# Lower parts of the second FFN's down weights: a negated ScalarE copy and an adding DMA in place of a VectorE subtraction

## The chip, the core and the metric

The kernel runs on one core of a Trainium2 chip. The metric is the device time of one execution in microseconds; lower is better. Three runs of the kernel before took 2208.71, 2209.5 and 2211.62 us; the median is 2209.5 us.

## What is computed

One layer of a diffusion backbone over 1024 latent tokens of width 1024, with 256 context tokens beside them: a half-step SwiGLU feed-forward, a parallel mixer (neighbourhood attention and an S5 scan), and a second half-step SwiGLU feed-forward. The last of these is what the change touches:

```
def swiglu(h, w_up, w_down):
    a, g = jnp.split(h @ w_up, 2, axis=-1)
    return (jax.nn.silu(g) * a) @ w_down
...
x = post_norm(x, 0.5 * mod[8] * swiglu(modulate(x, mod[6], mod[7]), ffn2_w_up, ffn2_w_down), ln_g[2], ln_b[2])
```

The hidden width is 2816, that is 22 blocks of 128; `w_down` is 2816 by 1024.

## The kernel before

TensorE multiplies in fp32r, and the kernel keeps float32 accuracy by writing each operand as an upper part (the value rounded to fp32r) and a lower part (what the rounding left). Each product of two such operands is three matmuls: upper by upper, upper by lower, lower by upper.

Weights arrive by DMA in units of 128 by 1024 (512 KB, tile `ws`). SP issues the loads; units rotate through three buffers (`NWS = 3`), and a buffer is loaded again once both of its halves have been split. A half (128 by 512) is an item. `w_split` makes its parts: ScalarE copies it into `wh` as fp32r (line 259), VectorE subtracts `wh` from the source into `wl` (line 261). `wh` and `wl` come from rings of four buffers. `take(n)` hands the next n items to TensorE and calls `w_split` so that `ahead[0]` items (normally four) are split, as far as the ring has room; then `w_next` issues the weight loads that have become possible. All of it is written in program order: every engine works its own list in order, and SP's list holds the loads and the stores of everything.

The down projection of the second feed-forward has 88 items, numbers `DOWN` to `DOWN + 87`, in two parts.

- Its first part works tokens 0 to 511. All eight PSUM banks accumulate (four token blocks by two halves of the columns). Each of the 22 hidden blocks takes two items and is 24 matmuls (lines 1793 to 1795: `h` by `wh`, `h` by `wl`, `l` by `wh`). The last two blocks go together, and four of their items have buffers of their own (`XE`). While it runs, SP also loads the hidden activations of both halves of the tokens (`hid_load`, line 1705), residual rows (line 1756) and rows of the norm (line 471). `take` for a block splits the two items of the block after it, since the ring has only four places.
- Its second part works tokens 512 to 1023 with `token_major`: first one half of the columns, then the other, one item and 12 matmuls a block (lines 397 to 399). During its first blocks VectorE finishes the first part: `updated` (lines 1771, 1772), the statistics (lines 420 to 426), the power on GpSimd (line 427), the norm (lines 436, 1776, 1777), after which SP stores the rows (line 1778). The last eight blocks of the second half of the columns go together (`TAIL = 8`), token block by token block; five of their items have buffers of their own (`XE`, `A`). Each token block is then finished at once and stored (lines 1771 to 1815).

GpSimd does almost nothing: 33 instructions in the whole kernel, in this stage only the powers of line 427. It issues no DMA.

Of the kernel before, what the change touches and what calls it, by code (L numbers as in the profile page):

```python
# [11 lines left out]
F32 = mybir.dt.float32  # L12
F32R = mybir.dt.float32r
I32 = mybir.dt.int32
AF = mybir.ActivationFunctionType
ALU = mybir.AluOpType
# [32 lines left out]
def hybrid_layer(ctx: ExitStack, tc: tile.TileContext, I, out, dbg=None, stop=99):  # L49
# [3 lines left out]
    V, S, G = nc.vector, nc.scalar, nc.gpsimd  # L53
# [12 lines left out]
    def nm(s):  # L66
        cnt[0] += 1
        return f"{s}_{cnt[0]}"
# [72 lines left out]
    units, items, last_use = [], [], {}  # L141
# [60 lines left out]
    DOWN = len(items)  # L202
# [23 lines left out]
    def w_dma(n):  # L226
        while pos[0] < min(n, len(units)):
            assert w_next(0)
# [3 lines left out]
    ready = {}  # L232


    def source(i, need=True):
        if i not in ready and i < len(items):
            u, f = items[i]
            if not need and (u >= pos[0] or i < U_ITEMS or i >= DOWN):
                return
            w_dma(u + 1)  # L240
            ready[i] = f()
        return ready.get(i)

    def w_split(n, must):
        while pos[1] < min(n, len(items)):
            i = pos[1]
            if i not in apart and len(ringed) >= 4:
                assert i >= must, i
                break
            if items[i][0] >= barred[0] and i >= must:  # L250
                break
            src = source(i)
            if i in apart:
                wh, wl = apart.pop(i)
            else:
                ringed.add(i)
                wh = wp.tile([128, 512], F32R, name=nm("wh"), tag="wh", bufs=4)
                wl = wp.tile([128, 512], F32R, name=nm("wl"), tag="wl", bufs=4)
            S.activation(wh, src, AF.Copy)  # L259
            source(i + 1, False)  # L260
            V.tensor_tensor(wl, ready.pop(i), wh.bitcast(F32), op=ALU.subtract)  # L261
            wsp[i] = (wh, wl)
            pos[1] += 1


    def take(n=1):
        i = pos[2]
        pos[2] += n
        for j in list(ringed):
            if j < i:  # L270
                ringed.discard(j)
        w_split(i + max(n, ahead[0]), i + n)
        while w_next(2):
            pass
        return [wsp.pop(j) for j in range(i, i + n)]
# [232 lines left out]
    for k in range(KD):  # L508
        if k + 2 < KD:
            k_load(k + 2)  # L510
        w_dma((2, 3, 4, 4, 4, 4, 5, 6)[k])
        for m in range(2):
            mod_tile(ws1.pop(0), m, k, True, False)
        if k == 0:
            for m in (1, 4, 7):
                V.tensor_scalar(bada[:, m], bada[:, m], 1.0, None, op0=ALU.add)
        V.tensor_tensor(modl[:, 0:2, k], modl[:, 0:2, k], bada[:, 0:2, k], op=ALU.add)
        if rest_of is not None:
            rest_of()
        w_split((0, 2, 4, 6, 8, 8, 8, 8)[k], 0)  # L520
        if k:
            grow(k - 1, (0, 1, 2, 3, 4, 4, 4, 4)[k])
        xt = xs.pop(0)
        S.activation(xt, xt, AF.Identity, scale=modl[:, 1, k:k + 1], bias=modl[:, 0, k:k + 1])
        S.activation(X[0][k], xt, AF.Copy)
        rest_of = lambda k=k, xt=xt: V.tensor_tensor(X[1][k], xt, X[0][k].bitcast(F32), op=ALU.subtract)
    rest_of()
    grow(KD - 1, 4)
    for i in range(8):
        wsp.pop(i)  # L530
    pos[2] = 8
    w_split(12, 0)
    started = ((pb8[0], pb8[1]), (pb8[2], pb8[3]))
    c_row(1)
# [1248 lines left out]
    for f in range(NF - LAST + 1):  # L1783
# [4 lines left out]
        for t in range(4):  # L1788
            for i in range(n):
                h, l = hidden(f + i, t)  # L1790
                for hf in range(2):
                    wh, wl = ws[2 * i + hf]
# [106 lines left out]
```

## Time and profile before

| | us |
|---|---|
| median of three runs | 2209.5 |
| lowest and highest run | 2208.71, 2211.62 |
| profiled execution, its own time | 2211.69 |
| profiled execution, span from the first to the last instruction | 2209.6 |
| TensorE busy in the span | 2154.9 (98%) |
| VectorE busy | 1597.0 (72%) |
| ScalarE busy | 739.1 (33%) |

The profiled execution lasts 2.1 us longer than its span and 2.2 us longer than the median of the runs. A matmul of 512 columns is listed with 0.39 us, but a new one starts every 0.227 us, since they are pipelined; the starts give the pace. The granted TensorE clock is a share of full speed.

### The profile page before, as it was taken

The numbers are of one execution on the slowest core, as the hardware profiler recorded it, in microseconds if no ns is written. First come the engines' busy times: TensorE is split into PE (matmuls) and PEld (weight loads), VectorE is DVE, ScalarE is ACT, GpSimd is POOL, SyncE is SP. The second block draws the span as 40 slices with busy tenths as digits, with TensorE's granted clock in tenths as the row PEclk, the third lists the DMA queues.
The fourth block names the chain that finished last, engine by engine and source line by source line (L and its number), as shares of the span: only waits on it lengthen the run. The fifth ranks groups of instructions, "written<-read, shape, count | busy, mean of one in ns | idle before, by whom it ended". The sixth has DMA issues, their size and how long they took to land. (4 is left out here: it accounts for less than half of the span.)

```text
span 2209.6 us, 32479 instructions
## 1 busy us (share of the span) xinstructions
PE 2154.9 (98%) x12272; PEld 1933.3 (87%) x12272; DVE 1597.0 (72%) x3425; ACT 739.1 (33%) x1547; POOL 22.0 (1%) x33
## 2 busy tenths in 40 slices
PE   6999999999999999999999999999899999999998
PEld 6998899889998999898899899986688888888786
DVE  7888878798887887553777466788877777744845
ACT  4322223423322223324222367634433333332121
POOL 0000000000000000000000000000000000000000
PEclk9999999999999999999999999999999999999999
DMA  9787723436433444433877675244223333279442
GB/s 353 251 291 258 268 67 109 161 100 237 128 124 117 126 135 128 137 125 128 274 252 248 179 175 136 81 168 162 103 108 114 115 114 115 96 266 390 168 150 83
DMA packets 169612, 372.31 MB, mean 169 GB/s; under 512 B 18152, under 2 KB 85736, under 8 KB 166640
## 3 DMA queue, kind: packets, MB, share of 16 engines
q1 hardware_dynamic: 169456, 370.25, 49.6%
q8 instruction: 96, 1.57, 0.3%
q14 instruction: 60, 0.49, 0.1%
HBM read 292.09 MB, written 84.06 MB: 170 GB/s over the span
## 5 line engine op out<-in xcount | busy, mean ns | idle before, releaser
L337 PE MATMUL pb<-X,wh 128*128 128x256 f32 (+2 forms) x1744 | 558.2, 320 | 0.9 <-ACT wh L259 0.9
L339 PE MATMUL pb<-X,wl 128*128 128x256 f32 (+2 forms) x1744 | 555.8, 319 | 0.0
L261 DVE TENSOR_TENSOR wl<-ws,wh 128x512 fp32r<-128x512 f32 x456 | 304.1, 688 | 246.8 <-ACT wh L259 241.3
L259 ACT ACTIVATE wh<-ws 128x512 fp32r<-128x512 f32 x456 | 278.7, 627 | 563.3 <-PE pb L399 288.0
L337 PEld LDWEIGHTS pb<-X,wh 128*128 128x128 f32 x1744 | 330.7, 190 | 9.6 <-ACT wh L259 1.3
L339 PEld LDWEIGHTS pb<-X,wl 128*128 128x128 f32 x1744 | 330.4, 189 | 8.7 <-DVE wl L261 0.4
L338 PE MATMUL pb<-X,wh 128*128 128x256 f32 (+2 forms) x946 | 306.8, 324 | 0.0
L338 PE MATMUL pb<-XT,wh 128*128 128x256 f32 (+2 forms) x886 | 283.3, 320 | 0.9 <-DVE XT L134 0.9
L397 PE MATMUL pb<-wh,HA 128*128 128x512 f32 x592 | 232.4, 393 | 2.0 <-DVE hid L366 1.4
L398 PE MATMUL pb<-wl,HA 128*128 128x512 f32 x592 | 230.5, 389 | 0.8 <-DVE wl L261 0.8
L338 PEld LDWEIGHTS pb<-X,wh 128*128 128x128 f32 x946 | 179.1, 189 | 7.1
L338 PEld LDWEIGHTS pb<-XT,wh 128*128 128x128 f32 x886 | 168.1, 190 | 6.4 <-DVE XT L134 1.8
L337 PE MATMUL pb<-HA,wh 128*128 128x512 f32 (+2 forms) x424 | 154.1, 364 | 0.6 <-ACT wh L259 0.6
L339 PE MATMUL pb<-HA,wl 128*128 128x512 f32 (+2 forms) x424 | 153.0, 361 | 0.0
L1642 DVE TENSOR_TENSOR z<-pb,z 128x512 f32<-128x512 f32 x154 | 106.1, 690 | 47.2 <-PE pb L339 43.8
L397 PEld LDWEIGHTS pb<-wh,HA 128*128 128x128 f32 x592 | 111.2, 188 | 26.0 <-DVE hid L366 2.3
L398 PEld LDWEIGHTS pb<-wl,HA 128*128 128x128 f32 x592 | 111.2, 188 | 23.5 <-DVE wl L261 1.2
L399 PE MATMUL pb<-wh,HA 128*128 128x512 f32 x336 | 130.9, 389 | 0.0
L338 PE MATMUL pb<-HA,wh 128*128 128x512 f32 (+2 forms) x336 | 118.7, 353 | 0.0
L399 PE MATMUL pb<-wh,HB 128*128 128x512 f32 x252 | 98.1, 389 | 0.0
L337 PEld LDWEIGHTS pb<-HA,wh 128*128 128x128 f32 x424 | 79.8, 188 | 11.5 <-ACT wh L259 1.1
L339 PEld LDWEIGHTS pb<-HA,wl 128*128 128x128 f32 x424 | 79.8, 188 | 10.6 <-DVE wl L261 0.4
(465 smaller groups left out, 3776.9 us busy)
## 6 DMA issues: line engine op xcount, KB each, us to landing
ws<-wu SPq DMA_DIRECT2D x122, 512.0 KB
ws<-wd SPq DMA_DIRECT2D x88, 512.0 KB
hd<-XE SPq DMA_DIRECT2D x22, 1024.0 KB
XE<-wada SPq DMA_DIRECT2D x36, 512.0 KB
HX<-wada SPq DMA_DIRECT2D x36, 512.0 KB
XE<-s5m SPq DMA_DIRECT2D x21, 768.0 KB
HA<-hd SPq DMA_DIRECT2D x20, 512.0 KB
HX<-wu SPq DMA_DIRECT2D x18, 512.0 KB
```

Of the source, the lines that this page charges most:

```text
L259: S.activation(wh, src, AF.Copy)
L261: V.tensor_tensor(wl, ready.pop(i), wh.bitcast(F32), op=ALU.subtract)
L337: mm(p, lhsT=wh, rhs=xh, start=first, stop=False)
L338: mm(p, lhsT=wh, rhs=xl, start=False, stop=False)
L339: mm(p, lhsT=wl, rhs=xh, start=False, stop=last)
L397: mm(b[t], lhsT=h, rhs=wh, start=f + i == 0, stop=False)
L398: mm(b[t], lhsT=h, rhs=wl, start=False, stop=False)
L399: mm(b[t], lhsT=l, rhs=wh, start=False, stop=f + i == nf - 1)
L1642: V.tensor_tensor(o, s[i][0], x, op=ALU.add)
```

## The change

An item of the down projection (`i >= DOWN`, 88 of them) no longer gets its lower part from VectorE. ScalarE copies the source a second time, scaled by -1 and rounded to fp32r, into `wl`. Then GpSimd issues a DMA from the source tile to `wl` that adds what it reads to what is there: source minus rounded source. The lower part is ready when that DMA has landed, and the source buffer is free then too. All other items keep the subtraction.

```
@@ w_split @@
+            u = items[i][0]
             src = source(i)
...
             S.activation(wh, src, AF.Copy)
-            source(i + 1, False)
-            V.tensor_tensor(wl, ready.pop(i), wh.bitcast(F32), op=ALU.subtract)
+            if i >= DOWN:
+                S.activation(wl, ready[i], AF.Copy, scale=-1.0)
+                G.dma_start(wl.bitcast(F32), ready.pop(i), accum_op=ALU.add)
+            else:
+                source(i + 1, False)
+                V.tensor_tensor(wl, ready.pop(i), wh.bitcast(F32), op=ALU.subtract)
             wsp[i] = (wh, wl)
```

## Rows read from the trace of the kernel before

**Rows 1.** The page: busy time of each engine and its share.

```profile
PE 2154.9 (98%) x12272; PEld 1933.3 (87%) x12272; DVE 1597.0 (72%) x3425; ACT 739.1 (33%) x1547; POOL 22.0 (1%) x33
```

**Rows 2.** Busy time by stretches of the down projection.

```profile
core 0: us, PE busy (x) PEld busy (x) DVE busy (x) ACT busy (x) POOL busy (x), PEclk, DMA share, GB/s
1966.00:2043.00 77.00, 77.00 (x341) 63.75 (x341) 31.84 (x39) 17.75 (x29) 0.00 (x0) 1.00 1.03 395
2043.00:2064.80 21.80, 21.80 (x98) 18.06 (x97) 13.76 (x17) 7.19 (x13) 0.00 (x0) 1.00 0.63 211
2075.70:2100.00 24.30, 20.95 (x88) 16.05 (x88) 23.82 (x38) 3.68 (x6) 3.16 (x4) 1.00 0.44 154
2110.00:2184.00 74.00, 74.00 (x328) 61.31 (x327) 28.95 (x45) 18.61 (x31) 0.00 (x0) 1.00 0.29 95
```

**Rows 3.** Waits of TensorE from 1940 to the end: total, times, longest.

```profile
PE pb L398 <- DVE wl L261: 3.4, 4, 0.9
```

**Rows 4.** Groups by form from 1961 to 2184, VectorE and ScalarE.

```profile
L259 ACT ACTIVATE wh<-ws 128x512 fp32r<-128x512 f32 x75 | 46.8, 631 | 167.5 <-PE pb L399 75.8 <-PE pb L1795 63.9 <-DMA ws<-wd 25.6
...
L261 DVE TENSOR_TENSOR wl<-ws,wh 128x512 fp32r<-128x512 f32 x76 | 51.7, 692 | 105.5 <-ACT wh L259 101.4 <-DMA ws<-wd 4.1
```

**Rows 5.** Timeline of SP, loads of the first part: start, duration.

```profile
1966.47 0.38 SPq L221 DMA_DIRECT2D ws<-wd  x1
...
1995.75 0.33 SPq L221 DMA_DIRECT2D ws<-wd  x1
1996.13 0.53 SPq L1705 DMA_DIRECT2D HA<-hd  x1
1997.29 0.52 SPq L1705 DMA_DIRECT2D X<-hd  x1
1998.53 0.33 SPq L471 DMA_DIRECT2D HX<-lnr  x1
```

**Rows 6.** Issues from 1966 to 2043 by line, the weight loads: count and size.

```profile
ws<-wd SPq DMA_DIRECT2D x15, 512.0 KB
```

**Rows 7.** Timeline of ScalarE, first part: start, duration, idle before.

```profile
1977.59 1.16 ACT L259 ACTIVATE wh<-ws 128x512 fp32r<-128x512 f32 x2 [2.70 <-DMA ws<-wd]
...
1988.24 1.31 ACT L259 ACTIVATE wh<-ws 128x512 fp32r<-128x512 f32 x2 [4.13 <-PE pb L1795]
1993.68 1.31 ACT L259 ACTIVATE wh<-ws 128x512 fp32r<-128x512 f32 x2 [4.13 <-PE pb L1795]
```

**Rows 8.** Timeline of TensorE, where a block begins, and a block later.

```profile
1994.16 0.39 PE L1793 MATMUL pb<-wh,HA 128*128 128x512 f32 x1
...
1999.60 0.39 PE L1793 MATMUL pb<-wh,HA 128*128 128x512 f32 x1
...
2000.51 0.39 PE L1794 MATMUL pb<-wl,HA 128*128 128x512 f32 x1
```

**Rows 9.** Waits of SP from 1955 to 2100: total, times, longest.

```profile
SPq L221 <- DVE wl L261: 45.9, 18, 4.4
```

**Rows 10.** The issues of the final stores: durations, first and last start.

```profile
L1815 SPq DMA_DIRECT2D out<-A x5: 332/333/357, 2189.4 to 2206.1; - x5
```

**Rows 11.** Timelines of ScalarE, GpSimd, TensorE, early second part.

```profile
2078.68 0.63 ACT L259 ACTIVATE wh<-ws 128x512 fp32r<-128x512 f32 x1 [12.97 <-PE pb L399]
...
2083.23 3.16 POOL L427 TENSOR_TENSOR rs<-rs,mhalf 128x1 f32<-128x1 f32 x4 [557.56 <-DVE mv L424]
...
2086.64 0.39 PE L397 MATMUL pb<-wh,X 128*128 128x512 f32 x1
2087.90 0.50 PE L398 MATMUL pb<-wl,X 128*128 128x512 f32 x1 [0.87 <-DVE wl L261]
```

**Rows 12.** Timelines of ScalarE and VectorE, the last eight blocks.

```profile
2175.70 0.63 ACT L259 ACTIVATE wh<-ws 128x512 fp32r<-128x512 f32 x1 [2.09 <-PE pb L399]
2176.24 2.18 ACT L259 ACTIVATE XE<-ws 128x512 fp32r<-128x512 f32 x4
...
2183.86 0.70 DVE L1771 TENSOR_TENSOR pb<-pb,row 128x512 f32<-128x512 f32 x1 [3.79 <-PE pb L399]
```

## The prediction

> **What bounds the kernel now.** I read the busy shares first, then the down projection in stretches, then who waits for whom, then the timelines of the engines that the change touches.
>
> TensorE is busy 98% of the span, VectorE 72%, ScalarE 33%, GpSimd 1% [rows 1]. In the down projection the picture is sharper: from 1966 to 2064.8 and from 2110 to 2184 TensorE is busy all the time, at the full granted clock, while VectorE works 41% of the first of these stretches (31.84 of 77.00 us) [rows 2]. So VectorE's subtractions are not what TensorE waits for. TensorE's waits say the same: it waited for a lower part only 4 times, 3.4 us in total, at most 0.9 us [rows 3]. These four lie early in the second part, where VectorE also finishes the first part; there TensorE is busy 20.95 of 24.30 us [rows 2]. That is all the change can win from a VectorE with less to do: 3.4 us, or 0.15% of 2209.5.
>
> One resource is full in the first part, and it is not an engine that computes: the DMA engines. From 1966 to 2043 their share is 1.03 (packets overlap a little) at 395 GB/s [rows 2]. SP issues four loads of 512 KB for each block of 24 matmuls: the weights, the hidden rows for both token halves, and a row of the residual or the norm [rows 5, 6]. A block takes 5.44 us: ScalarE's pairs start 5.44 us apart and so do the blocks on TensorE [rows 7, 8]. Four loads are 2.10 MB, which at 395 GB/s take 5.31 us. TensorE and the DMA engines are thus matched within 0.13 us a block, and loads stand in line: the weights issued at 1966.47 let ScalarE start at 1977.59, 11.1 us later [rows 5, 7].
>
> **The change part by part.**
>
> *Removed:* 88 subtractions on VectorE at 0.69 us [rows 4], 61 us of an engine that is not the bound. Gain: the four waits, at most 3.4 us [rows 3].
>
> *Added on ScalarE:* 88 copies of the same form as the first, 0.63 us [rows 4], 55 us. Hidden by TensorE's matmuls: ScalarE works 17.75 of 77.00 us in the first part and 18.61 of 74.00 us in the second [rows 2]. What isn't hidden is their place in the chain to the lower part, below.
>
> *Added on the DMA engines:* 88 transfers of 256 KB (0.262 MB). No row shows an adding DMA. The lower bound of what it takes from the engines is a plain transfer: 0.262 MB at 395 GB/s [rows 2] is 0.66 us. The upper bound: source and old value are both read, twice that, 1.33 us. I take 1.33, since the sum needs both operands, and a transfer that takes the place of two reads can hardly be as cheap as one; the rows show only plain transfers [rows 2]. The Trainium skill ("Collectives: The Full Stack", section "The bandwidth ceiling: the fold count and why AG ≠ RS ≠ AR") says that a reducing transfer costs twice a copying one because the two operands are two reads on one ring, not because the addition costs cycles; its estimate would be the upper bound, no run here shows it, and it speaks against the change.
>
> In the full stretch each block needs two such transfers: 5.31 + 1.33 = 6.64 us by the lower bound, 5.31 + 2.66 = 7.97 us by the upper, against 5.44. That is 1.20 or 2.53 us a block, and from the fourth block to the sixteenth, where the stretch ends at 2043 [rows 2], there are 13: 15.6 or 32.9 us. Some is absorbed by the queue: a weight load is issued 2.07 us after its pair of copies starts (1995.75 against 1993.68) and needed three blocks on, 14.25 us later; it takes 11.1 [rows 5, 7]. So 3.1 us come off: 12.5 or 29.8 us, and I take 30. The other loads that queue up are for later, but they stand ahead of the weights in SP's order, so they can't be skipped.
>
> *The chain in the first part.* Now the second lower part of a pair ends 2.04 us after ScalarE's start, as SP's issue right behind it shows [rows 5, 7]. After: four copies, some 2.4 us (a pair takes 1.31 [rows 7]), then the DMA. The next block needs it at its fifth matmul, 2000.51 for a ScalarE start of 1993.68 [rows 7, 8], less 0.2 us for the weight load ahead: 6.6 us. So a DMA that lands within 4.2 us of its issue costs nothing, and each microsecond more costs one a block. Lower bound of the landing: the last store, the same size with no other traffic, is issued at 2206.1 [rows 10] and the span ends at 2209.6: 3.5 us. Upper bound: 11.1 us, a load that waits behind all others. I take 4 to 5 while the engines are full, as GpSimd's transfers have a queue of their own but share the engines; this is at most 0.8 us a block and lies inside the 2.5 already counted. The three last pairs meet a share of 0.63 [rows 2] and cost nothing.
>
> *SP's queue.* A weight buffer is free when the DMA lands, not when VectorE ends. SP already waits for VectorE there 18 times, 45.9 us in total, at most 4.4 [rows 9]; that wait grows by some 5 us (2.4 + 5 against 2.04), with the hidden rows and residual rows behind it. While the DMA engines are the bound this shortens their queue and costs nothing more; alone, the weights would have 14.25 - 5.4 = 8.9 us, enough when the queue is short.
>
> *Early second part.* GpSimd's list is in order too. Four powers of the norm stand ahead of the DMA for the fifth item, and they run from 2083.23 to 2086.39 [rows 11]. ScalarE has that item's copies done by 2080 (its first starts at 2078.68), but the DMA leaves only at 2086.4 and lands at 2089.9 (3.5 us). TensorE needs it at 2086.87 (2086.64 + 0.23) and had it at 2087.90. So one stall of 3.0 us where there were four of together 3.4. Behind it, two pairs whose weights arrive late now pass through two copies and a DMA instead of one subtraction; I price these at 0 to 4 us, take 2.4, and get +2 net (bounds -0.4 to +4).
>
> *The last eight blocks.* Their first token block ends at 2183.6, just ahead of VectorE's evacuation at 2183.86 [rows 12]; it is 24 matmuls, so it begins at 2178.4, and the lower part of the eighth item is used at 2183.4. ScalarE starts the last six items at 2175.70; twelve copies at 0.55 (four took 2.18) [rows 12] end at 2182.3. With 3.5 us for the DMA it lands at 2185.8: 2.4 us late, and TensorE's work to the end is behind it. With 5 us it is 3.9. I take 3.
>
> *Rest of the second part.* One item per 2.72 us (half a block), three steps ahead: 8.2 us for two copies (1.3) and a DMA (3.5). Hidden; the DMA share is 0.29 [rows 2]. It costs once the landing passes 6.9 us.
>
> **Sum.** 30 + 2 + 3 = +35 us. On the profiled execution's own 2211.7 us that is 2246.7; that execution lies 2.2 us above the median, so 2244.5 for the median. With the lower bounds, 12.5 - 0.4 + 2.4 = +14.5: 2224. With the upper ones and the queue's 3.1 us not used, 33 + 4 + 4 = +41: 2250.5.
>
> **The rivals.**
>
> *Latency, not bandwidth (0.20).* The adding DMA lands late because it shares full engines, or GpSimd issues it slowly. It decides from 4.2 us on. For it: loads there take 11.1 us [rows 5, 7]. Against: its queue is its own. Halfway between 3.5 and 11.1, at 7.3 us, each of 18 pairs costs 3.1: 56 us; the tail costs 6.2 and the second part's start about 6: +68, 2277.
>
> *Hidden (0.14).* The extra traffic displaces only loads for later, and the DMA lands inside 4.2 us. Against it: one list on SP, and a margin of 0.13 us a block. What stays is the tail and the start of the second part: 2 to 5 us, 2211.5 to 2214.5. The Trainium skill ("DMA: Bandwidth & Descriptors", section "Anatomy of one DMA — SWDGE (gpsimd) path") gives 2.0 us plus bytes over 436 GB/s for a DMA from GpSimd, here an estimate of 2.6 us; by that rule this rival would be right on latency. No run here shows it, and the rows' 3.5 us [rows 10] is hidden as well; neither says anything about the full stretch.
>
> *Not slower (0.06).* VectorE's four stalls go [rows 3] and nothing replaces them: -3.4, 2206. The place is the fifth item of the second part, and it decides there: its DMA would have to land by 2086.87, 0.5 us after GpSimd is free [rows 11]. I see no way.
>
> The forecast, DMA engines as the bound, has 0.60.
>
> **How the numbers follow.** The likeliest case gives 2244.5, its own range 2224 to 2251. I leave out the not-slower case (0.06), about half of the hidden one (below 2217; some 0.08) and the far side of latency (above 2280; some 0.07): 2217 to 2280. About 0.2% (4.4 us) is what a measurement can tell from no change. Not slower falls within it, and so does some 0.04 of the hidden case; faster would need more than the 3.4 us there are to win: faster 0.02, same 0.09, slower 0.89.
>
> **What would show it.** In the changed profile: blocks of the first part between 6.6 and 8 us instead of 5.44, the DMA share at 1.0 to the end of that stretch, and TensorE waiting there for the adding DMA or for upper parts whose weights are late; one wait of about 3 us near 2087 plus the delay; 2 to 4 us at the start of the last eight blocks; VectorE 61 us less busy and ScalarE 55 us more. I am wrong if the blocks stay at 5.44 us (hidden), or if they exceed 8 us with DMA engines that aren't full (latency).

## The result and the profile after

The changed kernel takes 2277.85 us (median of four runs, 2277.09 to 2284.44) against 2210.56 us for the kernel before on the same chip: ratio 1.0311 over all runs, 95% interval 1.029 to 1.0333 (the medians alone give 1.0304). It is 3.1% slower, some 67 us, inside the predicted range and about twice the predicted loss of 35 us. The profiled execution took 2277.09 us with a span of 2275.3 us, 65.7 us more than the span before.

The page, busy time of each engine, answers [rows 1]:

```profile
PE 2178.0 (96%) x12272; PEld 1941.8 (85%) x12272; DVE 1538.6 (68%) x3337; ACT 782.6 (34%) x1635; POOL 98.4 (4%) x121
```

VectorE has 88 instructions and 58 us less, ScalarE 88 instructions and 43.5 us more, GpSimd 88 issues at 0.87 us more. TensorE runs the same 12272 matmuls and loses 2 points of its share. In the first part, by the first row below, TensorE is busy 139.5 of 172.0 us, so the loss is in waits and in the clock.

Busy time by stretches, after: the whole first part, the whole second part, then parts of them, for [rows 2]. The columns are those of [rows 2].

```profile
1952.80:2124.80 172.00, 139.52 (x532) 106.64 (x530) 30.70 (x32) 52.24 (x95) 40.00 (x46) 0.91 1.00 288
2124.80:2275.30 150.50, 125.29 (x529) 100.22 (x527) 48.33 (x74) 45.31 (x80) 42.91 (x48) 0.95 0.75 186
1966.00:2043.00 77.00, 62.70 (x236) 47.57 (x234) 9.80 (x8) 21.93 (x40) 17.39 (x20) 0.90 1.03 310
2043.00:2124.00 81.00, 67.67 (x260) 52.38 (x261) 17.57 (x20) 24.01 (x44) 19.13 (x22) 0.92 1.00 274
2150.00:2245.00 95.00, 83.35 (x355) 67.37 (x353) 7.75 (x12) 40.14 (x72) 30.31 (x36) 0.96 0.91 217
1964.90:1970.40 5.50, 5.50 (x13) 4.33 (x14) 0.00 (x0) 0.00 (x0) 0.00 (x0) 0.50 1.07 305
1971.00:1976.00 5.00, 5.00 (x24) 4.12 (x23) 0.00 (x0) 2.19 (x4) 1.74 (x2) 1.00 1.05 390
```

The first part takes 172.0 us from its first matmul to the first of the second part, where it took 119.8 (1955.9 to 2075.7 in the trace before): +52.2. The rest, to the end of the span, takes 150.5 where it took 133.8: +16.7. The sum is 68.9; the other 3.2 us come off before any changed instruction, since the powers near 1515 already run that much earlier. In the same 77 us as in [rows 2] TensorE now starts 236 matmuls instead of 341, the DMA engines are as full as before (1.03), and yet they move 310 GB/s instead of 395. The share stays at 1.00 to the end of the first part, where [rows 2] had 0.63, and at 0.91 in the second part, where it had 0.29.

TensorE's waits, from 1950 to 2262, answer [rows 3] (total, times, longest):

```profile
PE pb L1799 <- DMA wl<-ws: 30.7, 20, 3.3
PE pb L403 <- DMA wl<-ws: 13.0, 5, 6.9
PE pb L403 <- DMA XE<-ws: 2.4, 1, 2.4
PE pb L1799 <- DMA XE<-ws: 1.8, 2, 1.1
PE pb L403 <- DMA A<-ws: 0.3, 1, 0.3
```

All are waits for lower parts that the adding DMA (line 263) brings: 32.5 us in the first part, 15.7 us in the second. That doesn't make up 52.2. The rest is in the busy time: 139.52 us instead of 119.80 for the same matmuls, at a mean granted clock of 0.91 instead of 1.00, which by this estimate is worth at most 139.52 x 0.09 = 12.6 us; 22 restarts of the pipeline are in it too. The last two stretches above show the clock. After this wait of 3.27 us

```profile
1964.83 0.79 PE L1799 MATMUL pb<-wl,X 128*128 128x512 f32 x1 [3.27 <-DMA wl<-ws]
```

it is granted at 0.50, the 1.2 GHz level, for 5.5 us (13 matmuls), and a little later 24 matmuls go into 5.0 us at full clock.

One block of the first part, timelines of ScalarE, GpSimd and TensorE, after (start, duration, idle before). It answers [rows 7, 8]:

```profile
2016.92 0.63 ACT L260 ACTIVATE wh<-ws 128x512 fp32r<-128x512 f32 x1 [6.29 <-PE pb L1800]
...
2018.50 0.61 ACT L262 ACTIVATE wl<-ws 128x512 fp32r<-128x512 f32 x1
2024.32 0.63 ACT L260 ACTIVATE wh<-ws 128x512 fp32r<-128x512 f32 x1 [5.21 <-PE pb L1800]
...
2018.37 0.87 POOL L263 DMA_DIRECT2D wl<-ws  x1 [6.58 <-ACT wl L262]
2019.41 0.87 POOL L263 DMA_DIRECT2D wl<-ws  x1 [0.17 <-issue]
...
2025.66 0.50 PE L1799 MATMUL pb<-wl,HA 128*128 128x512 f32 x1 [0.52 <-DMA wl<-ws]
...
2028.35 0.74 PE L1799 MATMUL pb<-wl,HA 128*128 128x512 f32 x1 [1.73 <-DMA wl<-ws]
2028.89 0.63 PE L1800 MATMUL pb<-wh,HA 128*128 128x512 f32 x1
2029.32 0.63 PE L1798 MATMUL pb<-wh,HA 128*128 128x512 f32 x1
```

ScalarE waits for a place in the ring (TensorE's line 1800, which frees `wh`), copies four times, GpSimd sends the two DMAs at once, and TensorE uses the first result 7.3 us after its issue, the second 8.9 us after. Pairs now start 7.40 us apart instead of 5.44. Nobody in this chain waits for weights: ScalarE's releaser is TensorE. In the whole first part ScalarE waits 12.1 us for weights, where it waited 12.9 before. After the second wait the matmuls start 0.43 us apart, the lower clock again.

This block is one of middle length. Blocks of the first part take 5.44 to 12.82 us, 7.8 on average, and many come in twos, as the starts of ScalarE's pairs show:

```profile
1971.66 0.63 ACT L260 ACTIVATE wh<-ws 128x512 fp32r<-128x512 f32 x1 [9.42 <-PE pb L1800]
1977.11 0.63 ACT L260 ACTIVATE wh<-ws 128x512 fp32r<-128x512 f32 x1 [3.26 <-PE pb L1800]
1989.37 0.63 ACT L260 ACTIVATE wh<-ws 128x512 fp32r<-128x512 f32 x1 [10.06 <-issue]
1994.81 0.63 ACT L260 ACTIVATE wh<-ws 128x512 fp32r<-128x512 f32 x1 [3.25 <-issue]
```

A block that waits long for its lower parts gives those of the next block time to land: each of the seven longest blocks (9.2 to 12.8 us) is followed by one of 5.44 us without a wait; in all, 14 of the 22 blocks wait. For some of these copies the profile names no releaser ("issue"), but from 1960 to 2096 all of the pairs start 0.43 to 0.45 us ahead of TensorE's next block, whatever is named: they go by TensorE's progress.

The DMA groups from 1966 to 2043 (queue: packets, MB, share of 16 engines; then the issues, their size and median landing), and the queue of GpSimd's DMAs on the page, for the whole kernel:

```profile
q1 hardware_dynamic: 7295, 18.75, 66.0%
q0 software_dynamic: 2766, 5.04, 36.3%
wl<-ws POOLq DMA_DIRECT2D x20, 256.0 KB, 7.2
```

```profile
q0 software_dynamic: 12672, 23.07, 5.8%
```

The view of line 263 gives the landing in that stretch, then in the whole kernel:

```profile
DMA to landing us min/median/max: 3.7/7.2/9.1
DMA to landing us min/median/max: 3.3/6.1/10.6
```

The 5.04 MB that GpSimd's queue moved are 19.2 transfers; 36.3% of 77 us makes 1.45 us for each. The loads beside them move 18.75 MB in 66.0%, which is 50.8 us, or 0.71 us for 256 KB. An adding byte costs the engines about twice a plain one.

### The profile page after: what moved, and what is told of

It is laid out like the page before. It is cut to its first block, busy times and chain, and to the rows that moved or that the text cites. A ratio compares the mean times of both kernels' runs of the same rounds, so it can differ in the third digit from the quotient of the medians.

```text
span 2275.3 us, 32698 instructions
## 1 busy us (share of the span) xinstructions
PE 2178.0 (96%) x12272; PEld 1941.8 (85%) x12272; DVE 1538.6 (68%) x3337; ACT 782.6 (34%) x1635; POOL 98.4 (4%) x121
## 3 DMA queue, kind: packets, MB, share of 16 engines
q0 software_dynamic: 12672, 23.07, 5.8%
## 5 line engine op out<-in xcount | busy, mean ns | idle before, releaser
L266 DVE TENSOR_TENSOR wl<-ws,wh 128x512 fp32r<-128x512 f32 x377 | 250.2, 687 | 136.6 <-ACT wh L260 134.1
L1776 DVE TENSOR_TENSOR pb<-pb,row 128x512 f32<-128x512 f32 x16 | 11.2, 698 | 126.5 <-PE pb L404 95.6
L263 POOL DMA_DIRECT2D wl<-ws x79 | 68.6, 889 | 618.3 <-ACT wl L262 600.7
```

Source lines behind the costliest of these rows:

```text
L263: G.dma_start(wl.bitcast(F32), ready.pop(i), accum_op=ALU.add)
```

## The experiments

Seen from the result, three things could make the first part longer: **the bytes** (the DMA engines are full, and everything in SP's list comes later; forecast +30), **the chain** (with a ring of four places a pair is split one block ahead, and its two DMAs must land within 4.2 us, which they don't), and **the release** (a weight buffer comes free only when the DMA has landed, and SP's list stands still for it). The forecast counted the bytes alone, and held that the chain lies inside them. The rivals are that the chain or the release adds to them.

In the table "first part" runs from its first matmul to the first of the second part, and "rest" from there to the end of the span; both are of the profiled execution. Each ratio is to the kernel before on the same chip, whose median lay between 2209.19 and 2211.23 us.

| kernel | first part | rest | median us | ratio [95%] |
|---|---|---|---|---|
| before | 119.8 | 133.8 | 2210.56 | 1 |
| after | 172.0 | 150.5 | 2277.85 | 1.0311 [1.029, 1.0333] |
| e7_add: no DMA | 120.2 | 133.9 | 2211.85 | 1.0013 [1.0004, 1.0023] |
| e1_narrow: chain, few bytes | 143.9 | 138.9 | 2238.45 | 1.0135 [1.012, 1.015] |
| e3_shadow: bytes, no chain | 151.6 | 146.6 | 2252.59 | 1.0204 [1.0187, 1.0222] |
| e2_plain: copy, no addition | 146.0 | 144.4 | 2248.24 | 1.0175 [1.0158, 1.0192] |
| e5_nohid: fewer other loads | 159.8 | 149.2 | 2268.98 | 1.0268 [1.025, 1.0287] |
| e9_narrow_wh: e1, early release | 140.8 | 137.8 | 2237.62 | 1.0123 [1.0106, 1.0139] |
| e11_shadow_ws: e3, late release | 149.5 | 148.1 | 2254.07 | 1.0199 [1.0182, 1.0215] |
| e10_narrow_look: e1, look-ahead | 126.8 | 140.8 | 2222.24 | 1.0049 [1.0034, 1.0064] |
| e6_look: after, look-ahead | 167.1 | 155.0 | 2275.87 | 1.0304 [1.0283, 1.0325] |
| e13_look2: the same, fewer blocks | 159.3 | 154.5 | 2269.74 | 1.0267 [1.0252, 1.0283] |
| e4_second: second part alone | 119.8 | 154.3 | 2231.6 | 1.0104 [1.0089, 1.0119] |
| e14_late: last 32 items alone | 119.8 | 141.4 | 2218.24 | 1.0036 [1.0021, 1.005] |
| e8_three: three items alone | 119.8 | 134.5 | 2209.32 | 1.0001 [0.9992, 1.001] |
| e12_pool: three on GpSimd, no DMA | 119.8 | 133.9 | 2209.98 | 0.9999 [0.999, 1.0008] |

### The second copy without the DMA

VectorE adds the source to the negated copy; the rest is as in the changed kernel.

```
-                G.dma_start(wl.bitcast(F32), ready.pop(i), accum_op=ALU.add)
+                V.tensor_tensor(wl, ready.pop(i), wl.bitcast(F32), op=ALU.add)
```

> The negated copy on ScalarE stays; VectorE adds the source to it, in place of the adding DMA. Both theories (DMA engines full; lower part lands late) put all of the loss on the DMA: about 2210 us, within 5 us of before. If the second copy on ScalarE or its place in the chain costs something by itself, it shows here: the early second part and the last eight blocks could lose 1 to 3 us.

TensorE's waits, as in the view of [rows 3]:

```profile
PE pb L403 <- DVE wl L263: 3.4, 4, 0.9
```

But for the line numbers it is the row of [rows 3], and the time is 0.13% above that of before. So 88 more copies on ScalarE are close to free, and nearly all of the loss hangs on the DMA.

### The chain and the bytes, one without the other

Only 16 of 512 columns go through the adding DMA (8 KB instead of 256); the waits and their order stay:

```
-                G.dma_start(wl.bitcast(F32), ready.pop(i), accum_op=ALU.add)
+                G.dma_start(wl[:, 0:16].bitcast(F32), ready.pop(i)[:, 0:16], accum_op=ALU.add)
```

> As the changed kernel, but each adding DMA adds only 16 of its 512 columns (the rest of the lower part stays the negated rounded value): the same issue, wait and release of the buffer, with 1/32 of the bytes. Theory A, the DMA engines are the bound because of the bytes (1.4 us of all 16 engines for each): the first part goes back to blocks of about 5.5 us and the time to 2212 to 2222 us. Theory B, the fixed delay from issue to landing and the queue shared with the loads: landings stay at 5 to 7 us while the engines are full, and the time stays above 2250 us.

The other way round, VectorE's subtraction stays, and an adding DMA of full size goes to spare room that nobody reads (two small fills before the loop set it up):

```
+            if i >= DOWN + 4:
+                sc = [X2[:, 7168:7680], HB3[:, 3072:3584], XT3[:, 2048:2560]][i % 3]
+                G.dma_start(sc.bitcast(F32), wh.bitcast(F32), accum_op=ALU.add)
```

> VectorE subtracts as before. Beside it GpSimd adds each upper part of the down projection (all but the first four items) into a spare tile by DMA; nothing reads that tile, and no weight buffer waits for it. The traffic of the change without its chain. Theory A (bytes): the loads come late all the same, the first part grows by 30 us or more, 2245 us or more. Theory B (chain): about 2212 us.

The narrow kernel: the largest of TensorE's waits in the first part, and the issues of the adding DMA from 1966 to 2043 with their size and median landing:

```profile
PE pb L1799 <- DMA wl<-ws: 14.0, 10, 2.4
```

```profile
wl<-ws POOLq DMA_DIRECT2D x22, 8.0 KB, 5.2
```

The shadow kernel: waits of TensorE in the down projection, then of ScalarE:

```profile
PE pb L1799 <- ACT wh L260: 14.5, 10, 2.3
PE pb L402 <- DVE wl L262: 7.1, 4, 5.8
...
ACT wh L260 <- DMA ws<-wd: 134.1, 21, 17.8
```

The chain without the bytes costs 24.1 us in the first part (143.9 against 119.8), the bytes without the chain 31.8. The narrow kernel's 2238.45 us lies between what the two theories gave for it; the shadow kernel's is what the bytes alone were said to cost. The two losses together would be 55.9; the changed kernel lost 52.2. In the rest it is the same: 5.1 and 12.8 make 17.9, against 16.7.

They are two kinds of wait. In the shadow kernel TensorE waits for upper parts, because ScalarE waits for weights that SP's crowded queue brings late, 111.7 us in the first part alone. In the narrow kernel it waits for lower parts whose 8 KB land after a median of 5.2 us, beside loads that keep the DMA share at 0.86, where 4.2 us were allowed. The changed kernel has only the second kind in its first part: all of TensorE's waits are for lower parts, and ScalarE waits for weights no longer than before (12.1 us). So that the sums nearly agree doesn't show that its loss is made of both, and that 30 of its 52.2 us come from late weights is not shown. What its traffic changes there is the landing: 5.2 us at the median and 24.1 us lost with 8 KB, 6.1 and 26.2 with a plain copy (the next experiment), 7.2 and 52.2 with the addition. The forecast's step that put the chain under the bytes is wrong either way.

### Is it the addition or the transfer

The DMA copies instead of adding, with the same bytes:

```
-                G.dma_start(wl.bitcast(F32), ready.pop(i), accum_op=ALU.add)
+                G.dma_start(wl.bitcast(F32), ready.pop(i))
```

> As the changed kernel, but the DMA from GpSimd copies the source over the lower part and does not add (the lower part then holds the whole source, so the output is another one). Same issue, same chain, same size. If an adding transfer takes the engines twice as long as a copying one (1.4 against 0.7 us), the first part shrinks from 172 to about 145 to 150 us and the time to 2240 to 2250 us. If the addition costs the engines nothing beyond the bytes of a copy, it stays at 2270 to 2280 us.

GpSimd's DMA queue on its page, and the landing of its DMAs into `wl` from 1960 on:

```profile
q0 software_dynamic: 7040, 23.07, 2.7%
```

```profile
DMA to landing us min/median/max: 2.2/4.2/7.1
```

For 23.07 MB the addition takes twice the engine time (5.8% of a span against 2.7%). Its median landing in this view is 5.9 us instead of 4.2; from 1966 to 2043 it is 7.2 instead of 6.1. Without it the first part is 26 us shorter; with a plain copy it would still lose 26 us. This is the row that was missing when the price was chosen between 0.66 and 1.33 us.

### What stands beside it in the engines

The first part no longer loads the hidden rows of the second half of the tokens (`hid_load(1, ...)` goes, one load of 512 KB a block):

```
-        if 5 <= f:
-            hid_load(1, f - 5)
```

> The changed kernel without the loads of hidden rows for the second half of the tokens that run during the first part (17 loads of 512 KB; the second part then mostly reads the rows of the first half again, so its output is another one). Theory A (the engines' time is the bound in the first part): 17 x 1.33 = 22 us less, about 2255 us. Theory B (the chain from copy to landing sets the blocks): the queue is shorter but the chain is the same, 2268 us or more.

12.2 us come back (172.0 to 159.8), and not where loads are gone from full engines. From 1966 to 2043 the engines are about as busy (share 0.99) though they move less (281 GB/s instead of 310), the adding DMA lands after 7.2 us as before, and TensorE starts 239 matmuls instead of 236. From 2043 on the share falls to 0.93, the median landing to 5.5 us (from 6.8), and there the time is won. Theory A asked for 22 us less; the pace follows the landing, as theory B had it.

### The release of the weight buffer

The narrow kernel again, but the DMA reads `wh`, so that the weight buffer is free after ScalarE's second copy:

```
-                G.dma_start(wl[:, 0:16].bitcast(F32), ready.pop(i)[:, 0:16], accum_op=ALU.add)
+                ready.pop(i)
+                G.dma_start(wl[:, 0:16].bitcast(F32), wh[:, 0:16].bitcast(F32), accum_op=ALU.add)
```

> As the narrow kernel (the DMA adds 16 columns of 512), but it reads from the upper part and not from the weight buffer, so the buffer is free after ScalarE's second copy; TensorE still waits for the landing. The narrow kernel lost 24 us in the first part without the bytes. Theory C1 (the weight loads that wait for the landing in SP's list leave the DMA engines idle): the first part falls from 144 to about 125 us, the time to about 2218 us. Theory C2 (TensorE waits for lower parts that land late, whatever the loads do): 2232 us or more.

And the shadow kernel with the weight buffer as source, so that the buffer has to wait for the landing there too:

```
-                G.dma_start(sc.bitcast(F32), wh.bitcast(F32), accum_op=ALU.add)
+                G.dma_start(sc.bitcast(F32), sr, accum_op=ALU.add)
```

> VectorE subtracts as before; beside it GpSimd adds the weight buffer itself (not the upper part) into a spare tile by DMA. Nobody reads that tile, but the weight buffer now waits for the landing, as in the change. With the upper part as source the first part took 152 us and the time was 2252.6. C1: the buffer's wait adds to the bytes, 2265 us or more. C2: it changes little, 2248 to 2257 us.

Early release gives 140.8 instead of 143.9 in the first part and the same time within the intervals; late release gives 149.5 instead of 151.6, and again the same time. In these two kernels the release costs nothing that can be seen in the time. In the changed kernel SP does wait longer for the buffers, 185.5 us in 35 waits from 1950 on, where VectorE made it wait 107.9 us in 32 before, but nobody waits for SP in turn in the first part: from 1985 to 2043 ScalarE, which takes the weights, is not seen to wait for a load. There the wait is long and not on the path.

### More look-ahead

Four buffers that exist already (the `XE` tiles) are lent to every other block of the first part, and `take` splits six items ahead instead of four. First with the narrow DMA, then with the full one, then with the full one for blocks 3 to 15 only, because the last blocks need the same four buffers:

```
+    for f in range(3, NF - LAST, 2):        # third kernel: NF - LAST - 4
+        for j in range(2):
+            apart[DOWN + 2 * f + j] = apart[len(items) - 5 + f // 2 % 2 * 2 + j]
+    ahead[0] = 6
```

> The narrow kernel with the look-ahead of two blocks in the first part. C2: TensorE's waits for lower parts go, the first part falls from 144 to about 122 us, the time to about 2216 us. C1: the loads still wait for the landings, little changes, 2232 us or more.

> The changed kernel with items of every second block of the first part in four further buffers and a look-ahead of two blocks: a lower part has 5.4 us more to land. Theory A (bytes): the DMA engines stay full and the first part stays above 155 us; 2258 to 2275 us. Theory B (late landing): TensorE's waits for the adding DMA in the first part (31 us) go, about 2235 us or less.

> The changed kernel (full transfers) with the look-ahead of two blocks again, but only for blocks 3 to 15, so that the four buffers are free when the last four items of the first part need them (in the first trial TensorE lost 8.7 us there at one place). If the bytes alone hold the first part once lower parts have time to land, it comes to the 150 to 152 us of the two shadow kernels and the time to about 2258 us. If the look-ahead doesn't help as long as the engines are full, it stays at 160 us or more, 2268 to 2278 us.

The narrow kernel with look-ahead, from 1966 to 2043, as in [rows 2]:

```profile
1966.00:2043.00 77.00, 75.45 (x332) 62.01 (x332) 17.16 (x14) 34.06 (x63) 26.09 (x30) 1.00 1.04 352
```

With time to land, the narrow DMA's chain is hidden: 332 matmuls instead of 341, full clock, and 7.0 us of loss in the first part instead of 24.1. That is the side of C2, though not all of what it gave (122 us, 2216).

With the full bytes the first part falls from 172.0 to 159.3 with look-ahead in 13 of the blocks, and TensorE still waits 25.1 us for lower parts (32.5 without). But ScalarE's releaser is now another: from 1960 to 2110 it waits 87.6 us, 19 times, for weights, as in the shadow kernels. They eat up the look-ahead: the pair copied from 2029.44 on, which had waited for its weights, is the one that TensorE's block from 2037.59 on needs, 8.2 us later, where the same pair of the narrow kernel has 12.6 us. So once the chain has room, late weights do matter. The 150 to 152 us of the shadow kernels were not reached; the time of 2269.74 us is that of the other expectation (2268 to 2278). What makes the last 8 us is not shown. One candidate is the release, which was tried only without look-ahead: SP waits 93.1 us for landings there before it can load weights that are late.

The kernel with look-ahead up to the end won little, 4.9 us in the first part: TensorE waits 12.4 us for lower parts in these buffers, 6.6 us of it at once, where the last blocks need them too. And all three lose 2 to 4.5 us more in the second part, so none comes near the kernel before.

### The second part

The adding DMA only there, then only for the last 32 items:

```
-            if i >= DOWN:
+            if i >= DOWN + 2 * NF:              # second kernel: DOWN + 56
```

> The change only from item 44 on, that is in the second part; the first part's items go by VectorE. From the two traces the second part accounts for 17 us of the 66: both theories give about 2225 us (2220 to 2232). If the second part only suffered from what the first part leaves behind (late loads), it comes out under 2217.

> The change for items 56 to 87 only: the second part without its first twelve items, where stores, hidden rows and weights fill the DMA engines. With the whole second part it was 2231.6 (+22). If the loss there comes from late weights and late landings at its start, most of it goes: about 2216 us (5 to 8 us for the last eight blocks remain). If it is spread over the part, about 2224 us.

Where the second part begins, timelines of GpSimd, then of TensorE's waits, in the changed kernel, for [rows 11]; then TensorE's waits in the last eight blocks, for [rows 12]:

```profile
2132.27 3.15 POOL L432 TENSOR_TENSOR rs<-rs,mhalf 128x1 f32<-128x1 f32 x4 [14.08 <-DVE mv L429]
2135.37 3.55 POOL L263 DMA_DIRECT2D wl<-ws  x4
2150.89 0.86 POOL L263 DMA_DIRECT2D wl<-ws  x1 [11.97 <-PE pb L403]
...
2138.73 0.50 PE L403 MATMUL pb<-wl,X 128*128 128x512 f32 x1 [2.67 <-DMA wl<-ws]
2142.81 0.50 PE L403 MATMUL pb<-wl,X 128*128 128x512 f32 x1 [1.04 <-DMA wl<-ws]
2158.21 0.79 PE L403 MATMUL pb<-wl,HA 128*128 128x512 f32 x1 [6.95 <-DMA wl<-ws]
...
2240.20 0.50 PE L403 MATMUL pb<-wl,HA 128*128 128x512 f32 x1 [0.83 <-DMA wl<-ws]
2243.55 0.80 PE L403 MATMUL pb<-XE,HB 128*128 128x512 f32 x1 [2.39 <-DMA XE<-ws]
```

Alone, the second part loses 20.5 us, of which the last 32 items make 7.6; by difference some 13 belong to the first twelve, at the start of the part. The wait for the fifth item is where it was forecast, behind the four powers, and of the size forecast: 2.67 us (2.66 in e4_second) for 3.0. What was not forecast is the wait of 6.95 us at 2158.21. Its DMA is issued at 2150.89 and used 7.3 us later, and before that ScalarE waited 12 us for the weights. In e4_second, which comes there with the first part undisturbed, the same wait is 6.5 us. These are its rows of SP, ScalarE and GpSimd:

```profile
2090.37 1.42 SPq L221 DMA_DIRECT2D ws<-wd  x1
...
2099.56 0.63 ACT L260 ACTIVATE wh<-ws 128x512 fp32r<-128x512 f32 x1 [12.19 <-DMA ws<-wd]
...
2101.01 0.86 POOL L263 DMA_DIRECT2D wl<-ws  x1 [11.79 <-ACT wl L262]
```

The weights take 9.2 us from issue to ScalarE, the adding DMA another 7 from its issue to TensorE's start at 2108.13, and TensorE has nothing else to do. In the kernel before the same weights were late as well: issued at 2091.57, with SP behind the stores of the first part, and on ScalarE at 2097.34. But from there it was one subtraction of 0.69 us, and TensorE waited 0.82 us. Now the pair passes through a second transfer, on engines as full as those it came by. Matmuls at half clock follow here too, as in e14_late from 2185.3 to 2190.8 (granted 0.50, 14 matmuls).

### Can a part of it pay

[rows 3] showed 3.4 us of waits for VectorE early in the second part. Three items there (the sixth to the eighth) get the new way, all others the subtraction; and in a second kernel the same three get GpSimd's own subtraction, without a DMA:

```
-            if i >= DOWN:
+            if 2 * NF + 5 <= i - DOWN <= 2 * NF + 7:
...
+            (G if 2 * NF + 5 <= i - DOWN <= 2 * NF + 7 else V).tensor_tensor(wl, ready.pop(i), wh.bitcast(F32), op=ALU.subtract)
```

> The kernel before, with the change for three items only: numbers 49 to 51, which in the early second part make TensorE wait 0.83 us each behind VectorE's norm. GpSimd is free then and the DMA engines have room. If the landing takes 3.5 to 5 us there, these three waits go: 2.5 us less than before (0.1%), at the edge of what can be told. If the DMA or its wait delays the next weights, it is 0 to 3 us more.

> The kernel before, with the subtraction of items 49 to 51 on GpSimd instead of VectorE, no DMA. It aims at TensorE's waits of 0.83 us each in the early second part. If GpSimd's subtraction takes under 3 us and nothing else moves: 2.5 us less than before, 2206.7. If VectorE and GpSimd hold each other up there, 0 to 4 us more.

Both give the time of the kernel before within 0.1%. The three DMAs land after a median of 8.4 us, between the stores and loads of this stretch, and TensorE waits 1.89 us for one of them: the waits for VectorE are exchanged for one for the DMA. GpSimd's three subtractions take 5.37 us, and VectorE's work beside them gets slower; the last two rows are the same two forms after GpSimd has ended:

```profile
2083.53 5.37 POOL L262 TENSOR_TENSOR wl<-ws,wh 128x512 fp32r<-128x512 f32 x3
...
2086.00 1.77 DVE L437 TENSOR_SCALAR z<-z,mv,rs 128x1024 f32<-128x1024 f32 x1
2087.81 2.18 DVE L1777 TENSOR_TENSOR z<-z,HX 128x1024 f32<-128x1024 f32 x1
2091.17 0.81 DVE L437 TENSOR_SCALAR z<-z,mv,rs 128x1024 f32<-128x1024 f32 x1
2092.01 1.23 DVE L1777 TENSOR_TENSOR z<-z,HX 128x1024 f32<-128x1024 f32 x1
```

No version of the change that was run beats the kernel before.

## Why the prediction was half right

**What bounds the kernel, and *Removed*.** Right for the kernel before: VectorE lost 58 us of work, and the 3.4 us of waits for it were all there was to win. The forecast that the DMA engines, by weights that come late, bound the kernel after the change is not what its first part shows (below).

***Added on ScalarE.*** Right: 43.5 us on the page (55 were priced), 0.13% in e7_add.

***Added on the DMA engines.*** Right, and the upper price was nearly the true one: 1.45 us instead of 1.33. The bytes alone cost 31.8 us in the first part (29.7 in e11_shadow_ws) for a term of 30. The Trainium skill ("Collectives: The Full Stack", section "The bandwidth ceiling: the fold count and why AG ≠ RS ≠ AR") gives two reads on one ring as the reason why a reducing transfer costs twice a copying one. In size this trace agrees: 5.8% against 2.7% of the engines for the same 23.07 MB; the reason no run here shows.

***The chain in the first part.*** This is the step that failed, in two ways. Its size: "I take 4 to 5 while the engines are full", and the landing was 7.2 us at the median; even 8 KB took 5.2. A queue of its own was no protection: beside loads that took 66% of the engines' time the adding DMA landed after 7.2 us, in the second part beside loads that took 37% (2150 to 2245) after 4.3. And its place: the step "lies inside the 2.5 already counted", as if late weights set the pace and covered it. In the changed kernel they didn't: TensorE waited 32.5 us for lower parts and never for an upper one, and ScalarE waited for TensorE to free a place in the ring of four. [rows 7] had shown that releaser already. e1_narrow (24.1 us with few bytes), e5_nohid (fewer loads, the same pace while the landing stays the same) and e10_narrow_look (look-ahead hides it) agree. The step also left out that matmuls at half clock follow such waits, up to 12.6 us of the 52.2, and that the last pairs would meet full engines as well: the share stayed at 1.00 from 2043 on, with a wait of 2.65 us for one of them.

The rival *Latency, not bandwidth* gave 2277 us from a landing of 7.3 us and +56 in the first part; 7.2 and +52.2 were measured. It had the right wait. That its number fits so well is in part luck: 7.3 was the middle between two bounds, and its sum was 18 pairs at 3.1 us each. Measured were 32.5 us of waits in 14 of 22 blocks, since a long block lets the next pair land in time, and some 20 us of slow clock and restarts, which it didn't have. Its name is half wrong too: with few bytes the same chain costs 24 us, and it takes the bytes to bring the landing from 5.2 to 7.2 us. The mark that was to tell it from the forecast (blocks above 8 us on engines that aren't full) was no good either: blocks took 7.8 us on average, inside the forecast's 6.6 to 8, but singly 5.44 to 12.82, and the engines' share was 1.00 to 1.03 all the while.

The Trainium skill ("DMA: Bandwidth & Descriptors", section "Anatomy of one DMA — SWDGE (gpsimd) path") has the rule that gave the estimate of 2.6 us for a DMA from GpSimd. No run here shows that time for 256 KB that are added: in the changed kernel the shortest landed after 3.3 us, the median after 6.1. A copy came to 2.2 us at the shortest and 4.2 at the median. None was measured on engines with nothing else to do.

***SP's queue.*** Right as far as tried: e9_narrow_wh and e11_shadow_ws leave the time where it was.

***Early second part.*** The stall of the fifth item was right (2.67 for 3.0); one of 1.04 us came behind it, since the four DMAs issued there landed after up to 10.6 us, where 3.5 had been taken. The two late pairs were priced at "0 to 4 us"; one wait of 6.95 us and the clock after it came instead.

***Rest of the second part.*** Right but for one wait of 1.48 us: from 2165 to 2236 the landing was 4.1 us at the median and 6.5 at most, under the 6.9 that it named as its limit. And that although the share named as its cover, 0.29, had become 0.91, 0.54 of it from GpSimd's own queue.

***The last eight blocks.*** Waits of 0.83, 2.39 and 0.30 us, 3.5 together for the 3 taken, and some 2 us of half clock behind them, which no step had.

By terms: bytes +30 forecast, 30 to 32 measured alone, but as late weights that the changed kernel's first part doesn't have; chain 0 forecast, and it is what TensorE waited for in the 52.2 measured; second part +5 forecast, +16.7 measured. What stays open is how much of the 16.7 us is waits, clock and late weights item by item; only the sums over stretches were taken apart. Nor was a longer ring for the second part tried.

## What to carry to other kernels

Price a move onto the DMA engines twice: as bytes on the engines (an adding transfer counted double here), and as a landing time in the chain to its consumer, taken from rows in the same stretch and not from a quiet one, with the change's own bytes on top. Don't put the one price under the other: here the bytes made the landing longer, and look-ahead, which hid the landing of few bytes, left the late weights of the full ones. Look for what ties the producer to the consumer (here a ring of four places), since this decides whether a late transfer only shortens a queue or stops TensorE each time. And relief of an engine that nobody waits for is worth the waits in the trace, here 3.4 us, however busy it looks.

## What was not expected of the hardware

- TensorE's granted clock fell to 0.50 (the 1.2 GHz level) after waits of 1.7 to 7 us in the middle of a stage that had run at 1.00 in the kernel before, for up to 5.5 us: 13 or 14 matmuls instead of 24, about 2.5 us lost. It didn't follow every wait: after one of 2.67 us at 2138.73 in the changed kernel the matmuls kept the full pace. In e10_narrow_look, with hardly a wait from 1966 to 2043, it stayed at 1.00 there.
- The size of a transfer hardly set its landing in full engines: 8 KB took 6.0 and 6.6 us at the median (the two groups of e10_narrow_look from 1966 to 2043, share 1.04), 256 KB with the addition 7.2 (the changed kernel, share 1.03).
- A high share alone didn't make the landing long: 4.3 us at the median at a share of 0.91 in the second part, where most of the share was the adding transfers' own.
- Three subtractions on GpSimd, of 1.79 us each, went with VectorE's operations beside them taking 1.77 and 2.18 us instead of 0.81 and 1.23.
